# Re-cutting the token groups of a 1040-token input projection into 272, 256 and 512

## The chip, the core and the metric

One core of a Trainium2 chip runs the whole kernel as one program. Its engines are TensorE (PE in the profile; PEld is its weight load, which overlaps the matmuls), VectorE (DVE), ScalarE (ACT), GpSimd (POOL) and SyncE (SP); DVE and ACT do the elementwise work, SP and ACT issue the DMAs. The metric is device time of one execution in microseconds (us): the median of three runs of the kernel before is 1239.22 us (1239.05 to 1239.32).

## The reference

One layer of a hybrid decoder on 16 meta tokens plus 1024 tokens, float32, width 1024. What the change touches is the first product, `z`, and the way its results go on:

```
h = layer_norm(concat(meta, x))                       # 1040 x 1024
z = h @ w_in + b_in                                   # 1040 x 3840
q(512) | k(128) | v(128) | c_val(512) | c_gate(512) | g_attn(1024) | g_conv(1024) = split(z)
y_attn = sliding_window_attention(q, k, v, ...) @ w_attn_proj     # window 128, 16 meta keys, 8 heads, 2 kv heads
c = silu(layer_norm(causal_dwconv31(c_val * sigmoid(c_gate))));  y_conv = c @ w_conv_proj
mixed = sigmoid(g_attn) * y_attn + sigmoid(g_conv) * y_conv
h = layer_norm(ALPHA * h + mixed @ w_out)
u, g = split(causal_dwconv3(h @ ffn_w_up))            # 2 x 2816
out = layer_norm(ALPHA * h + (gelu(g) * u) @ ffn_w_down)[16:]
```

## The kernel before

**The product z.** Every large product is made with split operands: a float32 value is a high part, rounded to the format that TensorE multiplies, and a low part, the rest. One chunk of 128 inputs is three matmuls, high·high, high·low and low·high (lines 300, 304 and 305 in `product`). h0, the normalized input, is kept transposed and split in two arrays, RHO (input chunks 0 to 3) and RHC (4 to 7); `h0(k, hl, a, b)` gives the place of chunk k, part hl, tokens a to b. z has 30 column tiles of 128. The first three (k, v and the first query tile) are made in `z_first` while h0 is still being built; the other 27 go through `z_tile`: eight for the convolution (`conv_chunk`, two for each of four channel blocks), three query tiles, sixteen gate tiles. A tile walks three token groups, HG = 0 to 272, 272 to 656 and 656 to 1040; query and gate tiles use TG, where the first group starts at token 14 and has 258. A group is 8 chunks, 24 matmuls, into one PSUM buffer (`ps_z`, three of them), and is then evacuated: by ACT into a staging place in FA (`stage`: five slots of 400 columns) for gates and queries, by DVE (line 668) into `cin` for the convolution's values. The weights of a tile come by DMA and are split by ACT (line 269) and DVE (line 272).

**Queries.** `q_evac` stages a group, casts it to its high part `qsh` on ACT (line 354), subtracts it on DVE into the low part `qsl` (line 355) and stores both to DRAM (`qd`), the high part by ACT's queue, the low one by SP's. Attention loads them later as `qt`.

**What runs between.** From 55 to 410 us the z tiles share TensorE with attention (scores `ps_s`, transposes `ps_t`, outputs `ps_o`) and the sums of the convolution's layer norm (`ps_m`). DVE does the convolution's 31 taps (line 677), attention's softmax and the evacuations. The order on each engine is set at build time by a scheduler from priorities (`tc.cur_priority`, `rank`) and a few explicit edges (`after`); `ahead` is a z chunk behind which the first attention matmuls are put. After 410 us come the two projections (`ps_p`), the output product (`ps_w`), the ConvFFN's first product (line 1568, matmuls of 258 and 256 columns, weights in `ws` and in parts of RHO) and its second (line 1712, 512 columns). `FA`, `RHC`, `RHO` and `OB` are large arrays whose parts are given new uses as the program goes on.

Of the kernel before, what the change touches and what calls it, by code (L numbers as in the profile page):

```python
# [23 lines left out]
F = mybir.dt.float32  # L24
R = mybir.dt.float32r
AF = mybir.ActivationFunctionType
OP = mybir.AluOpType
AX = mybir.AxisListType

P = 128  # L30
D = 1024
KC = D // P
# [3 lines left out]
U0 = 14  # L36
U = T - U0
HD = 64
NH = 8
NKV = 2  # L40
CW = 512
KW = 208
# [11 lines left out]
HG = [(0, 272), (272, 656), (656, 1040)]  # L54
UG = [(0, 258), (258, 642), (642, 1026)]

PG = [(0, 258), (258, 514), (514, 770), (770, 1026)]


HW = 514  # L60
# [40 lines left out]
def tile_hybrid_layer(  # L101
# [3 lines left out]
    nc = tc.nc  # L105
    PSUM = bass.MemoryType.PSUM

    def dram(ap, offset, dims):
        return bass.AP(tensor=ap.tensor, offset=ap.offset + offset, ap=[list(d) for d in dims])

    def load(o, i):
        return nc.sync.dma_start(out=o, in_=i)
# [5 lines left out]
    def f32(ap):  # L118
        return ap.bitcast(F)
# [19 lines left out]
    arena = ctx.enter_context(tc.tile_pool(name="arena", bufs=1, side="left"))  # L139
    dpool = ctx.enter_context(tc.tile_pool(name="scratch", bufs=1, space=bass.MemoryType.DRAM))  # L140

    FA = arena.tile([P, 6144], F, name="FA")
    RHC = arena.tile([P, 8320], R, name="RHC")
    RHO = arena.tile([P, 8320], R, name="RHO")
    OB = arena.tile([P, 4 * U], F, name="OB")

    v1d = dpool.tile([NH, J_LEN], F, name="v1d")
# [3 lines left out]
    qd = dpool.tile([P, 2 * 4 * U], F, name="qd")  # L151
# [11 lines left out]
    pat = ps_stack.enter_context(tc.tile_pool(name="pat", bufs=1, space=PSUM, reuse_waits="tile"))  # L163

    qsp_stack = ExitStack()
    qsp = qsp_stack.enter_context(tc.tile_pool(name="qsp", bufs=2, side="right", reuse_waits="tile"))
    start = ExitStack()
    sp = start.enter_context(tc.tile_pool(name="start", bufs=1, side="right", reuse_waits="tile"))

# [83 lines left out]


    def h0(k, hl, a, b):
        g = next(g for g, x in enumerate(HG) if a < x[1])
        x, y = HG[g]
        i, n = (k % 4) * 2 + hl, y - x
        o = i * n + ((6144 if i else 0), 272, 3344)[g]
        return (RHO if k < 4 else RHC)[:, o + a - x:o + b - x]  # L260


    tc.cur_priority = RK_QKV
# [28 lines left out]
    chunks_done = []  # L292
# [15 lines left out]
    def z_group(wt, g, a, b, evac):  # L308
        hi, lo = wt
        ps = pat.tile([P, 512], F, name="ps_z", tag="mm", bufs=3)  # L310
        product(ps[:, :b - a], [(hi[:, k], lo[:, k], h0(k, 0, a, b), h0(k, 1, a, b)) for k in range(KC)])
        with rank(RK_EVAC):
            evac(g, a, b, ps[:, :b - a])

    def z_tile(fill, groups, evac, wt=None):
        wt = wt or weights([P, KC, P], fill)
        for g, (a, b) in enumerate(groups):
            z_group(wt, g, a, b, evac)

    def in_cols(m):  # L320
        return lambda raw: load(raw, w_z[m])

    TG = [(a + U0 if i == 0 else a, b) for i, (a, b) in enumerate(HG)]

    st_next = [0]

    def stage(n, lo=4104, cnt=5):
        i = st_next[0] % cnt
        st_next[0] += 1
        return FA[:, lo + i * 400:lo + i * 400 + n]  # L330

    tc.cur_priority = RK_QKV + 1000

# [11 lines left out]
    def q_at(i):  # L345
        return 8 * P * i + 16


    def q_evac(r):
        def evac(g, a, b, ps):  # L350
            t = stage(b - a)
            nc.scalar.activation(t, ps, AF.Identity, bias=qb[:, r:r + 1], scale=HD ** -0.5)
            h, l = (qsp.tile([P, 400], R, name=n, tag=n)[:, :b - a] for n in ("qsh", "qsl"))
            nc.scalar.copy(h, t)
            nc.vector.tensor_tensor(l, t, f32(h), OP.subtract)
            for hl, (put, x) in enumerate(((store, f32(h)), (load, f32(l)))):
                c = 0
                if g == 0:
                    c = 2
                    load(dram(qd, (hl * 4 + r) * 2, [[8 * U, P], [1, 2]]), x[:, :2])  # L360
                n = (b - a - c) // P
                i = (a - U0 + c) // P
                put(dram(qd, q_at(i) + (hl * 4 + r) * HD, [[8 * U, P], [4 * P, 2 * n], [1, HD]]),
                    x[:, c:].rearrange("p (n q) -> p n q", q=HD))
        return evac


    def in_order():
# [256 lines left out]
    wt_c1 = [weights([P, KC, P], in_cols(m)) for m in (11, 7)]  # L625
# [9 lines left out]
    ap = att.enter_context(tc.tile_pool(name="att", bufs=1, side="right", reuse_waits="tile"))  # L635
# [18 lines left out]
    def conv_chunk(c):  # L654
        sig = {}

        def g_evac(g, a, b, ps):
            sig[g] = stage(b - a)

            nc.scalar.activation(sig[g], ps, AF.Tanh, bias=bcol(10 + c), scale=0.5)  # L660
            nc.scalar.activation(sig[g], sig[g], AF.Identity, bias=half_, scale=0.5)

        z_tile(in_cols(10 + c), HG, g_evac, wt_c1[0] if c == 1 else None)
        cin = cp.tile([P, 16 + T], F, name="cin", tag="cin")
        nc.vector.memset(cin[:, 0:16], 0.0)

        def v_evac2(g, a, b, ps):
            nc.vector.scalar_tensor_tensor(cin[:, 16 + a:16 + b], ps, bcol(6 + c), sig[g], OP.add, OP.mult)

        z_tile(in_cols(6 + c), HG, v_evac2, wt_c1[1] if c == 1 else None)  # L670
        with rank(RK_CONV + c * 100):
            for j in range(TAPS):
                wc = cdw[:, j * CH + c:j * CH + c + 1]
                if j == 0:
                    nc.vector.tensor_scalar(acc[c], cin[:, j:j + U], wc, cdwb(c), OP.mult, OP.add)
                else:
                    nc.vector.scalar_tensor_tensor(acc[c], cin[:, j:j + U], wc, acc[c], OP.mult, OP.add)  # L677

    def gate_tile(i):
# [6 lines left out]

        z_tile(in_cols(14 + i), TG, gate_evac)

# [14 lines left out]
    for r in range(2):  # L703
        rows = slice(r * HD, (r + 1) * HD)

        def put(o, j, skew=1):
            load(o[rows], dram(vd, r * J_LEN + j, [[L8 - skew, HD], [2 * J_LEN, NH // 2], [1, o.shape[-1]]]))
# [13 lines left out]
    for q4 in range(2):  # L721
        ps = pat.tile([P, 512], F, name="ps_v4", tag="t", bufs=2)
        for i in range(4):
            c = NMETA + (q4 * 4 + i) * P
            nc.tensor.transpose(ps[:, i * P:(i + 1) * P], vT[:, c:c + P], ident)
        src = ps[:, :].rearrange("p (n g d) -> p n g d", g=2, d=HD)
        for g in range(NKV):
            hi, lo = (V[:, q4 * 4:q4 * 4 + 4, g, i] for i in range(2))
# [10 lines left out]
    for r in range(1, 4):  # L739
        z_tile(in_cols(r), TG, q_evac(r))  # L740

# [13 lines left out]
    tc.cur_priority = RK_Z - 500  # L755
    first_chunk = len(chunks_done)
    gate_tile(0)
    ahead = chunks_done[first_chunk + 2 * KC + 5]

    tc.cur_priority = RK_ATT  # L760

# [3 lines left out]
    for h in range(NH):  # L765
        g, r = divmod(h, 4)
        o = ps[:2, h * 16:(h + 1) * 16]
        after(nc.tensor.matmul(o, pairs0[g][:, 0, r, :], Kx[g][:, 0, 0:16], start=True, stop=False), ahead)
        nc.tensor.matmul(o, pairs0[g][:, 1, r, :], Kx[g][:, 0, 0:16], start=False, stop=True)
    s2 = ap.tile([P, NH, 16], F, name="s2")  # L770
    nc.vector.memset(s2, 0.0)
    w2 = s2[:2]
    nc.vector.tensor_tensor(w2, ps[:2, :P].rearrange("p (h m) -> p h m", m=16), biasq, OP.add)
# [27 lines left out]
    for g in range(NKV):  # L801
# [4 lines left out]
        hi, lo = (t[:16, g * 8:g * 8 + 8].rearrange("p (r q) -> p r q", r=4) for t in p2)  # L806
        nc.scalar.copy(hi, src)
        nc.vector.tensor_tensor(lo, src, f32(hi), OP.subtract)
    for g in range(NKV):
        o = po[:, g * 8:g * 8 + 8]  # L810
# [7 lines left out]
    def weights_out(blocks):  # L818
        a, n = 2 * blocks[0], 2 * len(blocks)
        ps = pat.tile([P, 512], F, name="ps_r", tag="t", bufs=2)  # L820
        nc.tensor.transpose(ps[:4 * n, :P], rall[:, a:a + n].rearrange("p n h -> p (n h)"), ident)
        t = ap.tile([24, P], F, name="rt", tag="rt", bufs=2)
        nc.scalar.copy(t[:4 * n], ps[:4 * n, :P])
        for h in range(NH // 2):
            store(dram(rd, 2 * h * S + a * HD, [[HD, n], [S, 2], [1, HD]]),
                  t[h:4 * n:4].rearrange("p (r q) -> p r q", r=2))
# [5 lines left out]
    for i in range(NB):  # L832
        for g in range(NKV):
            q = load_q(g, i) if i else q0[g]
            s = ap.tile([P, 2, 2, KW], F, name="s", tag="s", bufs=3)
# [5 lines left out]
            for u in range(2):  # L841
# [3 lines left out]
                for h in range(2):  # L845
                    o = ps[:, h * KW:h * KW + w]
# [20 lines left out]
            for h in range(2):  # L867
                for u in range(2):
                    j = h * 2 + u
                    x = s[:, h, u, first[u]:]  # L870
# [6 lines left out]
            for n, cols_of in ((P, (0, 80)), (80, (P, 0))):  # L877
                ps = pat.tile([P, 512], F, name="ps_t", tag="t", bufs=2)
                used = [u for u in range(2) if i or n == 80 or u]
                x = slice(used[0] * 256, 512)  # L880
                for u in used:
                    for h in range(2):
                        c = (u * 2 + h) * P
# [7 lines left out]
            for u in range(2):  # L891
                terms = [(V[:, i - 1 + u, g], P, pts[0])] if i or u else []
                terms.append((VA[:80, 2 * i + u, g], 80, pts[1]))
                x = slice(u * 256, u * 256 + 256)
# [171 lines left out]

    MX_AT = {2: (RHC, 0), 3: (RHC, 1), 6: (RHC, 2), 7: (RHC, 3), 0: (RHO, 0), 4: (RHO, 1), 1: (RHO, 2), 5: (RHO, 3)}

# [64 lines left out]
    for m in range(KC):  # L1133
        hi, lo = weights([P, KC, P], lambda raw: load(raw, w_ab[m]))

        def branch(i, g, tag, bufs):
            a, b = PG[g]
            ps = pat.tile([P, 512], F, name="ps_p", tag=tag, bufs=bufs)
# [6 lines left out]
        def merge(g, psa, psb):  # L1145
            a, b = PG[g]
            n = b - a
# [51 lines left out]
    def quadrant(sub, kk, h):  # L1199
# [3 lines left out]

    B_AT = [[(RHC, 6224), (RHO, 4112), (OA, 16), (RX, 48), (OA, 2096), (OA, 6224), (OA, 4144)],
            [(OC, 48), (OC, 2096), (OC, 4144), (OC, 6192), (RHC, 2096), (RHC, 48), (RHC, 4144)]]
    B11, B21, BT2, BT1, BT3, BT4, B22 = range(7)
# [153 lines left out]

    RING = [RHO[:, i * 1024:(i + 1) * 1024] for i in range(4)]
    RING += [None] * 4
    RING += [RHO[:, 6208 + i * 1024:6208 + (i + 1) * 1024] for i in range(2)]
    ring_next, W2 = [0], []
# [79 lines left out]
    ahead = []  # L1444
# [4 lines left out]
    for i in (3, 7, 2, -1, 6, 0, 4, 1, 5):  # L1449
# [4 lines left out]
        ahead = [None, (i, *rows)] if i == 3 else [(i, *rows)]  # L1454
# [83 lines left out]
    for c in range(FC):  # L1538
# [8 lines left out]
        for subs in passes:  # L1547
            last = subs == passes[-1]
            w_next = iter(range(7))
            a, b = SUB[subs[0]][0], SUB[subs[-1]][1]  # L1550
            i = max(a, 2)
# [96 lines left out]

    F_AT = [(RHC, 6208), (RX, 0), (RHC, 0), (RHO, 0), (RHO, 2048), (RHO, 4096)]
    W_DN = [(OC, 0), (OC, 2048), (OC, 4096), (OC, 6144), (RHC, 2048), (RHC, 4096), (RHO, 6144)]  # L1650

# [215 lines left out]
```

## Time and profile before

| | value |
|---|---|
| median of 3 runs | 1239.22 us (1239.05 to 1239.32) |
| the profiled execution | 1238.92 us |
| its span, first to last instruction | 1237.1 us |
| granted clock of TensorE, mean | 0.999 |
| matmuls | 8539 |
| z tiles of `z_tile` | 27, from 55 to 410 us |
| busy in 55 to 130 us (75): DVE, ACT | 71.2, 23.5 us |
| busy in 200 to 275 us (75): DVE, ACT | 71.2, 46.1 us |

A row of the timeline is the start in us, the length in us, the engine, the line, the operation, what it writes and reads, and its shape. The length of a matmul contains its way through the array; successive matmuls overlap, so that what one costs is the distance of the starts. In the groups view, the first number behind the bar is the busy time in us, the second the mean length in ns.

### The profile page before, as it was taken

The page shows a single profiled execution, that of the slowest core. Times are in us where ns is not written, and L with a number is a line of the kernel's source. Part 1 is how long each engine was busy: PE and PEld are TensorE (multiplying, and loading weights), DVE is VectorE, ACT ScalarE, POOL GpSimd, SP SyncE. Part 2 cuts the span into 40 slices and gives each one's busy share as a digit, 9 for nine tenths or more (in the row PEclk, how much of TensorE's full clock was granted, in tenths as well). Part 3 has the DMA queues.
Part 4 walks back from the last instruction along what each step waited for, and adds up shares of the span by engine and source line. Part 5 has one row for each costly group of instructions (what it writes and reads, how often), then busy time and mean ns, then how long its engine had stood idle before and what let it go on. Part 6 is the DMA issues. An engine that isn't in the chain of part 4 may idle for free.

```text
span 1237.1 us, 21709 instructions
## 1 busy us (share of the span) xinstructions
PE 1226.4 (99%) x8539; PEld 1167.6 (94%) x8539; DVE 1084.2 (88%) x1842; ACT 580.1 (47%) x1048; POOL 16.0 (1%) x25
## 2 busy tenths in 40 slices
PE   9999999999999999999999999999999999999997
PEld 8999999999999999888999999999999998888885
DVE  7899989999978798759899999998999986996697
ACT  7532336654255323344655555455454554544330
POOL 1000000000000010000000000000000000000000
PEclk9999999999999999999999999999999999999999
DMA  7297844412265555222155555554465468987722
GB/s 283 73 297 154 195 115 107 133 36 91 76 164 153 183 147 146 103 86 86 56 176 204 196 189 204 188 179 145 163 211 190 177 244 318 391 314 292 255 86 85
DMA packets 109024, 213.08 MB, mean 172 GB/s; under 512 B 31739, under 2 KB 48683, under 8 KB 108794
## 3 DMA queue, kind: packets, MB, share of 16 engines
q1 hardware_dynamic: 93002, 200.63, 49.2%
q10 hardware_dynamic: 15920, 11.07, 2.9%
q8 instruction: 67, 1.10, 0.4%
q14 instruction: 35, 0.29, 0.1%
HBM read 150.04 MB, written 62.70 MB: 172 GB/s over the span
## 4 chain that ended last, share of the span: by engine, by line
PE 97%; DVE 2%; ACT 0%; issue 0%; DMA 0%; DVEq 0%; SPq 0%
PE px L1568 14%; PE py L1568 9%; PE ps_x L1712 9%; PE ps_z L304 8%; PE ps_z L305 8%; PE ps_z L300 8%; PE ps_z L1712 7%; PE pw L1568 5%; PE pz L1568 5%; PE ps_p L300 2%; PE ps_p L304 2%; PE ps_p L305 2%; PE ps_w L300 2%; PE ps_w L305 2%; PE ps_w L304 2%; PE ps_z L524 2%
## 5 line engine op out<-in xcount | busy, mean ns | idle before, releaser
L677 DVE SCALAR_TENSOR_TENSOR FA<-cin,cols,FA 128x1026 f32<-128x1026 f32 x120 | 152.1, 1278 | 0.9
L305 PE MATMUL ps_z<-RHO,wlo 128*128 128x384 f32 (+2 forms) x324 | 104.1, 321 | 0.0
L300 PE MATMUL ps_z<-RHO,whi 128*128 128x384 f32 (+2 forms) x324 | 103.9, 321 | 0.0
L304 PE MATMUL ps_z<-RHO,whi 128*128 128x384 f32 (+2 forms) x324 | 103.9, 321 | 0.0
L305 PE MATMUL ps_z<-RHC,wlo 128*128 128x384 f32 (+2 forms) x324 | 103.8, 320 | 0.0
L304 PE MATMUL ps_z<-RHC,whi 128*128 128x384 f32 (+2 forms) x324 | 103.7, 320 | 0.0
L300 PE MATMUL ps_z<-RHC,whi 128*128 128x384 f32 (+2 forms) x324 | 103.6, 320 | 0.0
L269 ACT CAST whi<-wr 128x1024 fp32r<-128x1024 f32 x37 | 38.9, 1051 | 91.6 <-PE ps_z L304 71.6
L1377 ACT CAST RHO<-wr 128x512 fp32r<-128x512 f32 x92 | 55.4, 619 | 24.2 <-DVE wr L1395 11.5
L1378 DVE TENSOR_TENSOR RHO<-wr,RHO 128x512 fp32r<-128x512 f32 x92 | 61.9, 684 | 5.0 <-ACT RHO L1377 4.9
L300 PEld LDWEIGHTS ps_z<-RHO,whi 128*128 128x128 f32 x324 | 61.0, 188 | 0.1
L300 PEld LDWEIGHTS ps_z<-RHC,whi 128*128 128x128 f32 x324 | 61.1, 189 | 0.0
L305 PEld LDWEIGHTS ps_z<-RHO,wlo 128*128 128x128 f32 x324 | 61.0, 188 | 0.0
L304 PEld LDWEIGHTS ps_z<-RHO,whi 128*128 128x128 f32 x324 | 61.0, 188 | 0.0
L304 PEld LDWEIGHTS ps_z<-RHC,whi 128*128 128x128 f32 x324 | 61.0, 188 | 0.0
L305 PEld LDWEIGHTS ps_z<-RHC,wlo 128*128 128x128 f32 x324 | 60.9, 188 | 0.0
L1395 DVE TENSOR_TENSOR wr<-wr 128x512 f32<-128x512 f32 x88 | 60.0, 682 | 0.2
L272 DVE TENSOR_TENSOR wlo<-wr,whi 128x1024 fp32r<-128x1024 f32 x35 | 42.7, 1219 | 11.5 <-ACT whi L269 11.1
L684 ACT ACTIVATE FA<-ps_z,cols 128x384 f32<-128x384 f32 (+1 forms) x48 | 26.1, 543 | 47.6 <-PE ps_z L305 42.0
L1580 ACT COPY FA<-px 128x514 f32<-128x514 f32 (+2 forms) x23 | 13.1, 571 | 73.1 <-PE px L1568 73.0
L1377 ACT CAST ws<-wr 128x512 fp32r<-128x512 f32 x60 | 36.3, 619 | 19.1 <-DVE wr L1395 11.8
L1568 PE MATMUL px<-OA,RHO 128*128 128x258 f32 (+1 forms) x336 | 43.8, 279 | 0.0
(475 smaller groups left out, 3477.4 us busy)
## 6 DMA issues: line engine op xcount, KB each, us to landing
wr<-in_w_up_dram SPq DMA_DIRECT2D x44, 512.0 KB, 4.7
wr<-in_w_z_dram SPq DMA_DIRECT2D x30, 512.0 KB, 4.8
fd<-FA SPq DMA_DIRECT2D x44, 256.0 KB, 2.4
OB<-in_w_down_dram SPq DMA_DIRECT2D x19, 512.0 KB
qt<-qd SPq DMA_DIRECT2D x28, 256.0 KB, 4.5
sgd<-FA ACTq DMA_DIRECT2D x32, 192.0 KB, 2.9
td<-OB SPq DMA_DIRECT2D x12, 512.0 KB
sums<-fd SPq DMA_DIRECT2D x12, 512.0 KB, 7.0
```

Source lines behind the costliest of these rows:

```text
L269: ins = nc.scalar.copy(hi, raw)
L272: return (nc.vector if quick else nc.gpsimd).tensor_tensor(lo, raw, f32(hi), OP.subtract)
L300: ins = nc.tensor.matmul(ps, ah, bh, start=i == 0, stop=False)
L304: nc.tensor.matmul(ps, ah, bl, start=False, stop=False)
L305: last = nc.tensor.matmul(ps, al, bh, start=False, stop=i == n - 1)
L677: nc.vector.scalar_tensor_tensor(acc[c], cin[:, j:j + U], wc, acc[c], OP.mult, OP.add)
L684: nc.scalar.activation(t, ps, AF.Tanh, bias=bcol(14 + i), scale=0.5)
L1377: nc.scalar.copy(hi, src)
L1378: ins = nc.vector.tensor_tensor(lo, src, f32(hi), OP.subtract)
L1395: ins = nc.vector.tensor_tensor(*x)
L1568: ins = nc.tensor.matmul(o, x[:, ks], bmat(sub, q, hl, k), start=first and k + j == 0, stop=k == 3 and j == 2, skip_group_check=not first)
L1712: nc.tensor.matmul(banks[i], l[:, ts], r[:, ws], start=first and a and x + k == 0, stop=z and x == len(ops) - 1 and k == 2, skip_group_che ...
```

## The change

The 27 tiles of `z_tile` take the groups ZG = 0 to 272, 272 to 528 and 528 to 1040, so 272 (258 for gates and queries), 256 and 512; h0 is still built in HG, and the first three tiles still use HG. h0's slots are laid out anew: the second and third group of a chunk now stand behind each other (768 columns), the first group's slots begin at column 6196, and RHO and RHC grow from 8320 to 8384 columns. The staging in FA becomes one ring of 2040 columns that hands out just what is asked for. A query group beyond the first is cast, subtracted and stored in parts of at most 256 columns, from three buffers instead of two. s2 shares the ring of the scores `s`, `rt` has one buffer, and `ahead` is two chunks later.

```diff
@@ constants @@
+ZG = [(0, 272), (272, 528), (528, 1040)]
@@ tile_hybrid_layer @@
-    RHC = arena.tile([P, 8320], R, name="RHC")
-    RHO = arena.tile([P, 8320], R, name="RHO")
+    RHC = arena.tile([P, 8384], R, name="RHC")
+    RHO = arena.tile([P, 8384], R, name="RHO")
...
-    qsp = qsp_stack.enter_context(tc.tile_pool(name="qsp", bufs=2, side="right", reuse_waits="tile"))
+    qsp = qsp_stack.enter_context(tc.tile_pool(name="qsp", bufs=3, side="right", reuse_waits="tile"))
...
     def h0(k, hl, a, b):
-        g = next(g for g, x in enumerate(HG) if a < x[1])
-        x, y = HG[g]
-        i, n = (k % 4) * 2 + hl, y - x
-        o = i * n + ((6144 if i else 0), 272, 3344)[g]
-        return (RHO if k < 4 else RHC)[:, o + a - x:o + b - x]
+        i = (k % 4) * 2 + hl
+        o = 6196 + i * 272 if a < 272 else 16 + i * 768 - 272
+        return (RHO if k < 4 else RHC)[:, o + a:o + b]
...
-    TG = [(a + U0 if i == 0 else a, b) for i, (a, b) in enumerate(HG)]
+    TG = [(a + U0 if i == 0 else a, b) for i, (a, b) in enumerate(ZG)]
...
-    def stage(n, lo=4104, cnt=5):
-        i = st_next[0] % cnt
-        st_next[0] += 1
-        return FA[:, lo + i * 400:lo + i * 400 + n]
+    def stage(n):
+        o = st_next[0] if st_next[0] + n <= 2040 else 0
+        st_next[0] = o + n
+        return FA[:, 4104 + o:4104 + o + n]
...
             nc.scalar.activation(t, ps, AF.Identity, bias=qb[:, r:r + 1], scale=HD ** -0.5)
-            h, l = (qsp.tile([P, 400], R, name=n, tag=n)[:, :b - a] for n in ("qsh", "qsl"))
-            nc.scalar.copy(h, t)
-            nc.vector.tensor_tensor(l, t, f32(h), OP.subtract)
-            for hl, (put, x) in enumerate(((store, f32(h)), (load, f32(l)))):
...
+            cut = b - a if g == 0 else 256
+            for x in range(0, b - a, cut):
+                parts_of(r, g, t[:, x:min(b - a, x + cut)], a + x)
         return evac
+
+    def parts_of(r, g, t, a):
+        n = t.shape[-1]
+        h, l = (qsp.tile([P, 272], R, name=x, tag=x)[:, :n] for x in ("qsh", "qsl"))
+        nc.scalar.copy(h, t)
+        nc.vector.tensor_tensor(l, t, f32(h), OP.subtract)
+        for hl, (put, x) in enumerate(((store, f32(h)), (load, f32(l)))):
+            c = 0
+            if g == 0:
+                c = 2
+                load(dram(qd, (hl * 4 + r) * 2, [[8 * U, P], [1, 2]]), x[:, :2])
+            m = (n - c) // P
+            i = (a - U0 + c) // P
+            put(dram(qd, q_at(i) + (hl * 4 + r) * HD, [[8 * U, P], [4 * P, 2 * m], [1, HD]]),
+                x[:, c:].rearrange("p (n q) -> p n q", q=HD))
...
-        z_tile(in_cols(10 + c), HG, g_evac, wt_c1[0] if c == 1 else None)
+        z_tile(in_cols(10 + c), ZG, g_evac, wt_c1[0] if c == 1 else None)
...
-        z_tile(in_cols(6 + c), HG, v_evac2, wt_c1[1] if c == 1 else None)
+        z_tile(in_cols(6 + c), ZG, v_evac2, wt_c1[1] if c == 1 else None)
...
-    ahead = chunks_done[first_chunk + 2 * KC + 5]
+    ahead = chunks_done[first_chunk + 2 * KC + 7]
...
-    s2 = ap.tile([P, NH, 16], F, name="s2")
+    s2 = ap.tile([P, 2, 2, KW], F, name="s2", tag="s", bufs=3)
+    s2 = s2.rearrange("p a b c -> p (a b c)")[:, :NH * 16].rearrange("p (h m) -> p h m", m=16)
...
-        t = ap.tile([24, P], F, name="rt", tag="rt", bufs=2)
+        t = ap.tile([24, P], F, name="rt", tag="rt", bufs=1)
```

TensorE at the first z tile of the convolution, where its first group ends and its second begins, before:

```order
L300 MATMUL ps_z<-RHC,whi 128x272
L304 MATMUL ps_z<-RHC,whi 128x272
L305 MATMUL ps_z<-RHC,wlo 128x272
L300 MATMUL ps_z<-RHO,whi 128x384
L304 MATMUL ps_z<-RHO,whi 128x384
L305 MATMUL ps_z<-RHO,wlo 128x384
```

The same place in the changed kernel:

```order
L299 MATMUL ps_z<-RHC,whi 128x272
L303 MATMUL ps_z<-RHC,whi 128x272
L304 MATMUL ps_z<-RHC,wlo 128x272
L299 MATMUL ps_z<-RHO,whi 128x256
L303 MATMUL ps_z<-RHO,whi 128x256
L304 MATMUL ps_z<-RHO,wlo 128x256
```

And 24 matmuls further on there, where the third group begins (before, a second group of 384 begins at this place):

```order
L299 MATMUL ps_z<-RHC,whi 128x256
L303 MATMUL ps_z<-RHC,whi 128x256
L304 MATMUL ps_z<-RHC,wlo 128x256
L299 MATMUL ps_z<-RHO,whi 128x512
L303 MATMUL ps_z<-RHO,whi 128x512
L304 MATMUL ps_z<-RHO,wlo 128x512
```

The number of matmuls of the tile and their order in it are the same; the widths of the second and third group differ.

ACT at the second group of the first query tile, while h0 is being built (L480 and L488 are the scaling and the cast to the high part of h0's chunks, L352 the query's evacuation, L354 its cast, L343 the evacuation of k), before:

```order
L352 ACTIVATE FA<-ps_z,qb 128x384
L488 CAST RHO<-tm 128x384
L354 CAST qsh<-FA 128x384
L480 ACTIVATE tm<-ps_h_526,cols 128x384
L480 ACTIVATE tm<-ps_h_527,cols 128x384
L116 DMA qd<-qsh 128x6x64
L343 ACTIVATE FA<-ps_z,cols 128x384
L488 CAST RHC<-tm 128x384
L480 ACTIVATE tm<-ps_h_528,cols 128x384
```

The same place now (the lines have moved by 5 to 6, evacuations by −1: L485 for L480, L493 for L488, L360 for L354, L351 for L352):

```order
L351 ACTIVATE FA<-ps_z,qb 128x384
L493 CAST RHO<-tm 128x384
L360 CAST qsh<-FA 128x256
L360 CAST qsh<-FA 128x128
L485 ACTIVATE tm<-ps_h_532,cols 128x384
L485 ACTIVATE tm<-ps_h_533,cols 128x384
L117 DMA qd<-qsh 128x4x64
L117 DMA qd<-qsh 128x2x64
L342 ACTIVATE FA<-ps_z,cols 128x384
L493 CAST RHC<-tm 128x384
L485 ACTIVATE tm<-ps_h_534,cols 128x384
```

One cast more stands ahead of the scaling of the last chunks of h0, and one DMA issue more ahead of k's evacuation.

More of the change, by code (lines that the diff above doesn't have):

```diff
@@ L352, in evac @@
             nc.scalar.activation(t, ps, AF.Identity, bias=qb[:, r:r + 1], scale=HD ** -0.5)
-            h, l = (qsp.tile([P, 400], R, name=n, tag=n)[:, :b - a] for n in ("qsh", "qsl"))
-            nc.scalar.copy(h, t)
-            nc.vector.tensor_tensor(l, t, f32(h), OP.subtract)
-            for hl, (put, x) in enumerate(((store, f32(h)), (load, f32(l)))):
[L357 to L364, printed above, removed]
-        return evac
+            cut = b - a if g == 0 else 256
+            for x in range(0, b - a, cut):
+                parts_of(r, g, t[:, x:min(b - a, x + cut)], a + x)
+        return evac
+    def parts_of(r, g, t, a):
[12 more added lines that the diff above has]
+                x[:, c:].rearrange("p (n q) -> p n q", q=HD))
     def in_order():
```

## The prediction

> **What bounds the kernel now.** I read the page first (busy times, clock, chain), then the waits of PE, the windows by stage, and last the timeline and the longest pieces of the chain for the price of one matmul.
>
> ```profile
> PE 1226.4 (99%) x8539; PEld 1167.6 (94%) x8539; DVE 1084.2 (88%) x1842; ACT 580.1 (47%) x1048; POOL 16.0 (1%) x25
> PEclk9999999999999999999999999999999999999999
> PE 97%; DVE 2%; ACT 0%; issue 0%; DMA 0%; DVEq 0%; SPq 0%
> PE ps_w L548 <- DVE sel L1101: 1.1, 1, 1.1
> PE ps_h L474 <- ACT xn L440: 0.6, 1, 0.6
> PE pw L1568 <- DVE OA L1253: 0.4, 1, 0.4
> PE ps_z L521 <- ACT FA L480: 0.3, 1, 0.3
> ```
>
> TensorE is busy for 1226.4 of 1237.1 us at the full clock in all forty slices, makes 97% of the chain that ended last, and has four waits in all, 2.4 us together. None of them lies between 55 and 410 us, where the 27 z tiles stand that the change touches. There the windows say:
>
> ```profile
> 55.00:130.00 75.00, 75.00 (x485) 74.57 (x484) 71.22 (x85) 23.51 (x40) 0.00 (x0) 1.00 0.78 208
> 130.00:200.00 70.00, 70.00 (x487) 69.43 (x486) 65.22 (x133) 28.90 (x83) 0.00 (x0) 1.00 0.58 151
> 200.00:275.00 75.00, 75.00 (x545) 74.59 (x545) 71.20 (x174) 46.11 (x138) 0.00 (x0) 1.00 0.34 92
> 335.00:410.00 75.00, 75.00 (x487) 75.00 (x486) 60.59 (x122) 38.91 (x60) 0.00 (x0) 1.00 0.58 161
> ```
>
> The columns after the length are PE, PEld, DVE, ACT and POOL. PE is never idle; DVE has 3.8, 4.8, 3.8 and 14.4 us free. So what counts is the time from the start of one matmul to the start of the next ("start to start"), and after that whether DVE can follow a faster PE.
>
> **The group sizes.** Each of 27 tiles has three token groups of 24 matmuls; two groups of 384 become one of 256 and one of 512, and the 258 (272 in the eight conv tiles) stays. The instruction count and the streamed columns stay the same, so a gain can come only from what a matmul costs beyond its columns. First rows of three successive groups, and the groups with the new widths elsewhere in the program:
>
> ```profile
> 364.67 0.34 PE L300 MATMUL ps_z<-RHO,whi 128*128 128x384 f32 x1
> 368.83 0.34 PE L300 MATMUL ps_z<-RHO,whi 128*128 128x384 f32 x1
> 373.35 0.28 PE L300 MATMUL ps_z<-RHO,whi 128*128 128x258 f32 x1
> 376.25 0.34 PE L300 MATMUL ps_z<-RHO,whi 128*128 128x384 f32 x1
> 376.43 0.34 PE L304 MATMUL ps_z<-RHO,whi 128*128 128x384 f32 x1
> ...
> 627.30 2.72 PE px L1568 x24
> 632.74 2.79 PE px L1568 x24
> 1019.41 29.93 PE ps_z L1712 x132
> ...
> L1568 PE MATMUL px<-OC,RHO 128*128 128x256 f32 x312 | 39.6, 276 | 0.0
> L305 PE MATMUL ps_z<-RHO,wlo 128*128 128x384 f32 x216 | 73.2, 339 | 0.0
> ```
>
> The 24 matmuls of 384 take 368.83 − 364.67 = 4.16 us, 173.3 ns each. The 24 of 256 in the FFN's piece at 627.30 take 2.72 us, 113.3 ns each. The 132 of 512 take 29.93 us, 226.7 ns each. Beyond one column per cycle at 2.4 GHz (the 160.0, 106.7 and 213.3 that I reckon with) these are 13.3, 6.6 and 13.4 ns: the narrow one pays half. Two of 384 cost 346.6, a 256 and a 512 cost 340.0: 6.6 ns less. Six rows like the last one, x216 each, are 1296 matmuls of 384, thus 648 pairs: 648 × 6.6 = **−4.3 us**.
>
> The Trainium skill's page "TensorE: Matmul & The Clock Gate", section "Back-to-back issue gap", gives the isolated gap of a warm matmul as N/2.4 plus about 2.5 ns, the same extra for every width. By that rule 256 and 512 cost just what 384 and 384 cost, the term is 0 instead of −4.3, and the time would be 1240.0, 0.8 above before. The trace does not agree on the extra: it shows 13.3 at 384 and 6.6 at 256.
>
> **What a change of width gives back.** In the row pair 376.25 and 376.43 the first 384 after a 258 takes 180 ns by the printed starts, some 7 over the steady 173. No row shows 258, then 256, then 512 in z. For 27 × 3 changes of width at 0 to 20 ns I allow 0 to 1.6 us and take **+0.5**.
>
> **The new places in RHO and RHC.** The first group's slots move from 6144 to 6196 plus multiples of 272, those of the wider groups to 16 plus multiples of 768. Whether the start column matters can be bounded with the 258s: in z 24 of them take 376.25 − 373.35 = 2.90 us, 120.8 ns each, while the piece at 632.74 (258 wide too, with operands elsewhere) takes 116.3. If the new slots bring that price, 456 × 4.5 = −2.1 us. If they are the worse ones, I take the reverse, +2.1. Nothing says which, and the true start columns of before (62, 14, 30 and 46 modulo 64) and of after (50, 2, 18 and 34) interlace, so I take **−0.3**.
>
> **The query parts and the start.** A query group is cast, subtracted and stored in parts of at most 256 columns: one more part for each of the three late query tiles, two more for the first one, which is on its way while h0 is still being built.
>
> ```profile
> 40.38 0.53 ACT L354 CAST qsh<-FA 128x384 fp32r<-128x384 f32 x1
> 49.30 0.79 PE L524 MATMUL ps_z<-RHC,whi 128*128 128x384 f32 x2
> 49.64 0.19 PEld L524 LDWEIGHTS ps_z<-RHC,whi 128*128 128x128 f32 x1 [0.32 <-DVE RHC L491]
> L354 ACT CAST qsh<-FA 128x384 fp32r<-128x384 f32 x8 | 4.1, 517 | 0.2
> L354 ACT CAST qsh<-FA 128x258 fp32r<-128x258 f32 x4 | 1.6, 410 | 0.1
> L355 DVE TENSOR_TENSOR qsl<-FA,qsh 128x384 fp32r<-128x384 f32 x8 | 4.4, 553 | 1.5 <-DMA qd<-qsl 1.5
> L355 DVE TENSOR_TENSOR qsl<-FA,qsh 128x258 fp32r<-128x258 f32 x4 | 1.7, 420 | 0.0
> L116 ACTq DMA_DIRECT2D qd<-qsh x12: 366/372/428, 24.1 to 137.5; - x12
> ```
>
> By the two widths a cast of 256 and one of 128 take about 0.41 + 0.30 us against 0.52 (+0.19), the subtracts 0.42 + 0.28 against 0.55 (+0.15), and one more store is issued on ACT's queue (0.37). Behind them on ACT and DVE stand the casts and subtracts of the last h0 chunks (L488, L491), and for the last chunk PE does wait: the row at 49.64 names DVE RHC L491. So the extra work lands on the path there, in part: 0 to 0.7 us, I take **+0.3**. For the three late query tiles it is 0.19 us on ACT and 0.15 on DVE each, beside 3.8 us of idle DVE in that window: 0. The third qsh/qsl buffer, the shared s ring, the single rt buffer and `ahead` change no work; their cover is the slack below.
>
> **Interrupted groups.** Attention's transposes stand between z matmuls and interrupt some 256 groups, whose price after a transpose no row isolates. I allow 0 to 0.6 us, and take **+0.3**.
>
> **Who can follow.** The evacuations cost the same in sum (three per tile). The waits nearest to PE are these:
>
> ```profile
> 76.73 1.01 DVE L668 SCALAR_TENSOR_TENSOR cin<-ps_z,cols,FA 128x272 f32<-128x272 f32 x2
> 78.65 0.29 PE L300 MATMUL ps_z<-RHO,whi 128*128 128x272 f32 x1
> ...
> 343.67 1.23 DVE L928 TENSOR_TENSOR kx<-csum,c_hi 128x1026 fp32r<-128x1026 f32 x1 [1.12 <-ACT c_hi L927]
> 350.03 0.42 DVE L974 TENSOR_TENSOR FA<-FA,ps_m 128x258 f32<-128x258 f32 x1 [5.13 <-PE ps_m L921]
> ...
> 411.14 0.35 DVE L1025 CAST OA<-OB 128x384 fp32r<-128x384 f32 x1
> 414.00 0.28 PE L300 MATMUL ps_p<-OA,whi 128*128 128x256 f32 x1
> ```
>
> At 78.65 PE takes a ps_z buffer whose evacuation (the first of the two at 76.73) was done 1.4 us before; three tiles further on PE will be about 0.5 us early, which fits. At the means ps_m DVE finished 5.1 us before PE and then waited for it. At 414.00 PE uses a part of OA that was cast 2.5 us before, while DVE in that stretch is itself fed by PE. From the projection on the order of both kernels is the same, so what is saved by 410 us is kept to the end. I count 0.
>
> **Sum.** −4.3 + 0.5 − 0.3 + 0.3 + 0.3 = **−3.5 us**. The profiled execution took 1238.92 us, 0.3 under the median of 1239.22, so it becomes 1235.4, and the median 1239.22 − 3.5 = **1235.7**. A difference of 0.2% (2.5 us) is about what a measurement of this kernel can tell from no change: faster means under 1236.7, slower over 1241.7.
>
> **Rivals.**
>
> ```profile
> 591.50 1.58 PE L1568 MATMUL px<-OC,W 128*128 128x256 f32 x12
> 592.91 1.58 PE L1568 MATMUL pz<-OC,W 128*128 128x256 f32 x12
> 594.33 1.58 PE L1568 MATMUL px<-OC,RHO 128*128 128x256 f32 x12
> ...
> L1568 PE MATMUL px<-OC,ws 128*128 128x256 f32 x204 | 25.9, 276 | 0.0
> L1568 PE MATMUL pz<-OC,RHO 128*128 128x256 f32 x144 | 18.3, 276 | 0.0
> ```
>
> *The 256s stay slow.* Right behind a stretch of 512s the 24 matmuls from 591.50 to 594.33 take 2.83 us, 117.9 ns each, and they keep that for the whole stretch. In the changed z every 256 stands behind a 258 that stands behind 512s. Then 648 × 4.6 = 3.0 us go, and −0.5 is left: **1238.7**. Against it: the FFN, where 256s stand among 258s, has 113.3. Chance 0.15.
>
> *Every width pays the same extra in z.* The 258s of z pay 13.3 ns (120.8 − 107.5) like the 384s. With 120.0 for a 256, 648 × 6.7 = 4.3 us go, and the small losses stay: **1240.0**. Against it: the 113.3 of the FFN's piece. Here lands the rule of the skill as well. Chance 0.06.
>
> *DVE becomes the bound in attention.* It has 3.8 of 75 us free from 200 to 275 us. By 275 us PE is early by 220/355 of 4.3, 2.7 us; if DVE gives none of its free time, that part is lost: **1238.4**. For it: the 95% busy. Against it: much of DVE's work there waits for PE's scores and transposes, so its idle time moves too. Chance 0.04.
>
> *Slower: the FFN's weights lie worse.* RHO grows by 64 columns, and what is packed behind it moves with its parts. Nine rows from px<-OC,RHO x312 to pz<-OC,RHO x144 are 1596 matmuls of 256 in the FFN that read weights there. If the new place puts them at 117.9 instead of 113.3, 1596 × 4.6 = +7.3 and the sum is +3.8: **1243.0**; it decides against the gain from 3.5/1596 = 2.2 ns each. Against it: weights in RHO and in ws cost the same mean, 276. Chance 0.07.
>
> **How the numbers follow.** The forecast has 0.68; its own range, with the slot term from −2.1 to +1.0 and the small losses from nothing to their upper ends, is 1233.6 to 1237.2, and some 0.63 of the 0.68 lies under 1236.7. The rivals at 1238.7, 1240.0 and 1238.4 are within 0.2%, together 0.25. The range 1233.6 to 1240.0 leaves out the slow FFN (0.07) and some 0.05 at both ends. Faster 0.64 (that 0.63 and 0.01 of the DVE case, should it lose less), same 0.28 (0.05 of the forecast, the three rivals, less 0.02 given to either side), slower 0.08 (the FFN's 0.07 and that 0.01).
>
> **What would show it.** Right: 256 groups of z take 2.72 us from first to first row, 512 groups 5.44, tiles 11.0 instead of 11.2; PE's busy time falls by about 3.5 us with no new wait from 55 to 410 us; the FFN pieces stay at 2.72 and 2.79. Wrong: 256 groups of 2.83 us or more; 258 groups off 2.90 by over 0.1; a wait for DVE in the list of PE's waits; FFN pieces of 2.83.

## The result and the profile after

The changed kernel takes 1237.44 us in the median (22 runs, 1237.09 to 1239.56) against 1239.23 for the kernel before: 1.8 us less, a ratio of 0.9987 with a 95% interval of 0.9981 to 0.9993. So it is faster, clear of the interval, by about half of the 3.5 us that were forecast. By the limit that the prediction itself set (under 1236.7 us, 0.2% below before) it is "same", to which it gave 0.28, and not "faster". The execution profiled first was its slowest, 1239.56 us, and lost that time at the start; a second profile of the same kernel (called "again" below) took 1237.57. The windows of the first 55 us, for the kernel before, that first profile and again; the last numbers are the granted clock, the DMA share and GB/s:

```profile
0.00:55.00 55.00, 52.98 (x316) 49.25 (x317) 43.80 (x105) 37.30 (x67) 5.31 (x21) 1.00 0.53 183
```

```profile
0.00:55.00 55.00, 52.17 (x305) 48.59 (x306) 41.47 (x104) 35.91 (x65) 5.31 (x21) 0.97 0.50 171
PE ps_h L479 <- ACT xn L445: 1.4, 1, 1.4
```

```profile
0.00:55.00 55.00, 52.40 (x314) 49.07 (x314) 43.21 (x105) 36.99 (x68) 5.31 (x21) 1.00 0.51 178
PE ps_h L479 <- ACT xn L445: 1.2, 1, 1.2
PE 1224.6 (99%) x8539; PEld 1139.4 (92%) x8539; DVE 1085.1 (88%) x1847; ACT 580.5 (47%) x1053; POOL 15.9 (1%) x25
```

In the first profile TensorE was granted 0.97 there and its first z_tile matmul started at 57.9 us; again it started at 56.1, before at 55.5. So the middle of the program is read from again. PE's busy time in it is 1224.6 instead of 1226.4 us: 1.8 less, as the medians say. PEld falls from 1167.6 to 1139.4 us, which is no gain of its own: a weight load of z takes 188 ns in the mean in both profiles, but between the matmuls of 512 the loads no longer overlap one another.

The windows of again, for the four stretches that were shown of before and for the FFN's first product:

```profile
55.00:130.00 75.00, 75.00 (x496) 68.17 (x496) 72.62 (x91) 24.37 (x43) 0.00 (x0) 1.00 0.78 213
130.00:200.00 70.00, 70.00 (x483) 64.04 (x482) 64.18 (x131) 28.05 (x83) 0.00 (x0) 1.00 0.58 149
200.00:275.00 75.00, 75.00 (x543) 70.39 (x543) 72.89 (x178) 45.63 (x131) 0.00 (x0) 1.00 0.34 92
335.00:410.00 75.00, 75.00 (x491) 68.66 (x490) 61.41 (x123) 39.13 (x60) 0.00 (x0) 1.00 0.55 164
605.00:1019.00 414.00, 413.63 (x3590) 413.26 (x3589) 388.51 (x635) 223.09 (x367) 0.00 (x0) 1.00 0.52 184
```

and the last of these stretches in the kernel before:

```profile
605.00:1019.00 414.00, 413.62 (x3591) 413.30 (x3591) 389.04 (x635) 224.26 (x368) 0.00 (x0) 1.00 0.52 183
```

PE is still never idle from 55 to 410 us, and DVE is busier from 200 to 275 (72.9 of 75 us) without becoming the bound. The first product of the FFN keeps its pace: 3590 matmuls in the window, 3591 before. From the first matmul of the projections to the end it is 830.0 us in again and 830.1 before, so what z saves is kept.

What the groups cost, by the first rows of successive groups of again: a tile without interruption, the next tile's start, the first 512s of the tile in detail, and a 256 group in attention's stretch. A group is called undisturbed when no other matmul stands between its 24. The rows are printed to 0.01 us, so a price from one group is good to some 0.4 ns.

```profile
315.00 0.29 PE L299 MATMUL ps_z<-RHO,whi 128*128 128x258 f32 x1
317.88 0.28 PE L299 MATMUL ps_z<-RHO,whi 128*128 128x256 f32 x1
320.60 0.39 PE L299 MATMUL ps_z<-RHO,whi 128*128 128x512 f32 x1
326.10 0.29 PE L299 MATMUL ps_z<-RHO,whi 128*128 128x258 f32 x1
...
320.60 0.39 PE L299 MATMUL ps_z<-RHO,whi 128*128 128x512 f32 x1
320.83 0.39 PE L303 MATMUL ps_z<-RHO,whi 128*128 128x512 f32 x1
321.06 0.39 PE L304 MATMUL ps_z<-RHO,wlo 128*128 128x512 f32 x1
321.29 0.39 PE L299 MATMUL ps_z<-RHO,whi 128*128 128x512 f32 x1
...
277.61 0.28 PE L299 MATMUL ps_z<-RHO,whi 128*128 128x256 f32 x1
280.43 0.40 PE L299 MATMUL ps_z<-RHO,whi 128*128 128x512 f32 x1
```

The 256s take 2.72 us, 113.3 ns each, as forecast. The 512s take 5.50 us, 229.2 ns each, not 226.7; the three of a chunk take 0.69 us (320.60 to 321.29). And the 256 group at 277.61 takes 2.82 us, 117.5 each: the dearer price that 256s have behind the output product exists here too. In again 16 of the 27 groups of 256 have a median distance of starts of 113 or 114 ns and 11 one of 117 or 118; all the slow ones but one start between 150 and 305 us, where attention's matmuls stand between.

Added up over all their starts, the matmuls of z_tile take 307.1 us before (258s 55.6, 272s 24.5, 384s 227.0) and 304.7 in again (55.0, 24.5, 256s 75.3, 512s 149.9). Attention's scores, transposes and outputs take 0.5 us more than before. Between the first z_tile matmul and the first of the projections lie 351.5 us before and 349.7 in again.

### The profile page after: what moved, and what is told of

It reads as the page before. It is cut to its first block, busy times and chain, and to the rows that moved or that the text cites. A ratio compares the mean times of both kernels' runs of the same rounds, so it can differ in the third digit from the quotient of the medians.

```text
span 1237.7 us, 21739 instructions
## 1 busy us (share of the span) xinstructions
PE 1226.3 (99%) x8539; PEld 1140.5 (92%) x8539; DVE 1084.8 (88%) x1847; ACT 580.9 (47%) x1053; POOL 16.0 (1%) x25
## 4 chain that ended last, share of the span: by engine, by line
PE 97%; DVE 2%; ACT 0%; DMA 0%; issue 0%; SPq 0%; DVEq 0%; ACTq 0%
PE px L1574 14%; PE py L1574 9%; PE ps_x L1718 9%; PE ps_z L304 8%; PE ps_z L303 8%; PE ps_z L299 8%; PE ps_z L1718 7%; PE pw L1574 5%; PE pz L1574 5%; PE ps_p L299 2%; PE ps_p L304 2%; PE ps_p L303 2%; PE ps_w L303 2%; PE ps_w L299 2%; PE ps_w L304 2%; PE ps_z L529 2%
## 5 line engine op out<-in xcount | busy, mean ns | idle before, releaser
L304 PE MATMUL ps_z<-RHO,wlo 128*128 128x256 f32 (+2 forms) x324 | 103.5, 320 | 0.0
L303 PE MATMUL ps_z<-RHO,whi 128*128 128x256 f32 (+2 forms) x324 | 103.4, 319 | 0.0
L304 PE MATMUL ps_z<-RHC,wlo 128*128 128x256 f32 (+2 forms) x324 | 103.4, 319 | 0.0
L303 PE MATMUL ps_z<-RHC,whi 128*128 128x256 f32 (+2 forms) x324 | 103.4, 319 | 0.0
L299 PE MATMUL ps_z<-RHO,whi 128*128 128x256 f32 (+2 forms) x324 | 103.3, 319 | 0.0
L299 PE MATMUL ps_z<-RHC,whi 128*128 128x256 f32 (+2 forms) x324 | 103.2, 319 | 0.0
L1383 ACT CAST RHO<-wr 128x512 fp32r<-128x512 f32 x92 | 55.4, 619 | 23.1 <-DVE wr L1401 12.0
L1586 ACT COPY FA<-px 128x514 f32<-128x514 f32 (+2 forms) x23 | 13.1, 571 | 73.0 <-PE px L1574 72.9
L689 ACT ACTIVATE FA<-ps_z,cols 128x258 f32<-128x258 f32 (+2 forms) x48 | 26.1, 544 | 39.4 <-PE ps_z L304 36.6
L1384 DVE TENSOR_TENSOR ws<-wr,ws 128x512 fp32r<-128x512 f32 x60 | 40.4, 684 | 4.1 <-ACT ws L1383 4.0
```

Of the source, the lines that this page charges most:

```text
L299: ins = nc.tensor.matmul(ps, ah, bh, start=i == 0, stop=False)
L303: nc.tensor.matmul(ps, ah, bl, start=False, stop=False)
L304: last = nc.tensor.matmul(ps, al, bh, start=False, stop=i == n - 1)
L689: nc.scalar.activation(t, ps, AF.Tanh, bias=bcol(14 + i), scale=0.5)
L1384: ins = nc.vector.tensor_tensor(lo, src, f32(hi), OP.subtract)
```

## The experiments

All were run in the same manner as the changed kernel, with the kernel before beside them (1239.2 us each time); a time is the median of 11 executions, of 6 at column 8. Diffs are against the changed kernel. A start is named by its column in a period of 64 (256 bytes): by the addresses in the built program RHO and RHC themselves begin at column 48 of it, so that 16 + 768i is column 0. That the period is 64 is read from the 258s, whose prices repeat every four slots (4 × 272 is 17 × 64).

**The same kernel again.**

> The changed kernel once more, for a second profile of it (the first one has its TensorE clock at 0.97 over the first 55 us). Expected 1237.4 us, within 0.4. In z the 24 matmuls of 512 should again take 5.50 us (229.1 ns each: 226, 229, 232 in turn), those of 256 mostly 2.72. If the forecast's price of 226.7 for a 512 were right and the first profile odd, 5.44 us and the same time.

Measured 1237.36 us (ratio 0.9986, 0.9977 to 0.9995), and the 5.50 us just shown. The forecast's price of a 512 did not hold in z.

**The group sizes alone undone.**

```diff
-ZG = [(0, 272), (272, 528), (528, 1040)]
+ZG = [(0, 272), (272, 656), (656, 1040)]
```

> The group sizes alone undone: 272 (258), 384 and 384, with the new slots, ring and query parts. Theory A, the sizes bring the gain and the rest next to nothing: 384s at 173 to 175 ns again, 1239.0 us (before, less 0.6 for the 258s' slots, and 0.4 for the start). Rival B, the gain comes from the slots, the ring or the third buffer: 1237.4 us stays, or less.

Measured 1238.91 us (0.9999, 0.9991 to 1.0008), as theory A said, and the first rows

```profile
387.24 0.34 PE L299 MATMUL ps_z<-RHO,whi 128*128 128x384 f32 x1
391.40 0.34 PE L299 MATMUL ps_z<-RHO,whi 128*128 128x384 f32 x1
395.56 0.28 PE L299 MATMUL ps_z<-RHO,whi 128*128 128x258 f32 x1
```

give 4.16 us again, 173.3 ns for a 384. Beside the other edits the sizes bring 1.5 us; what those edits bring alone, 0.3 us, is within the interval.

**The wide slots at column 48.**

```diff
-        o = 6196 + i * 272 if a < 272 else 16 + i * 768 - 272
+        o = 6196 + i * 272 if a < 272 else i * 768 - 272
```

> The wide groups' slots start at 768i instead of 16 + 768i, so that their rows start 48 columns into the period of 64, where the 512s of the later products start, instead of 0. Theory A, the start column sets the price of a 512 in z: 226.7 instead of 229.1 ns, 648 x 2.4 = -1.6 us, 1235.9 us. Rival B, it is the two weights and three products of a chunk, or what stands between: the 512s stay at 229 and the time at 1237.4.

Measured 1239.46 us (1.0003, 0.9994 to 1.0012): 2.1 us slower than the changed kernel. The rows show both halves of it:

```profile
387.98 0.28 PE L299 MATMUL ps_z<-RHO,whi 128*128 128x256 f32 x1
390.85 0.40 PE L299 MATMUL ps_z<-RHO,whi 128*128 128x512 f32 x1
396.32 0.28 PE L299 MATMUL ps_z<-RHO,whi 128*128 128x258 f32 x1
...
395.19 0.39 PE L303 MATMUL ps_z<-RHC,whi 128*128 128x512 f32 x1
395.41 0.39 PE L304 MATMUL ps_z<-RHC,wlo 128*128 128x512 f32 x1
395.64 0.39 PE L299 MATMUL ps_z<-RHC,whi 128*128 128x512 f32 x1
395.87 0.39 PE L303 MATMUL ps_z<-RHC,whi 128*128 128x512 f32 x1
```

Three steps of the 512s from 395.19 to 395.87 take 0.68 us, 226.7 each, as theory A said. But the first six of such a group are dearer, some 231 ns in the mean, so that the whole group takes 5.47 us, 227.9 each, and over all starts the 512s save 0.6 us (149.9 to 149.3) of the 1.6 expected. And the 24 matmuls of 256 now take 2.87 us, 119.6 each, all over z (the median distance is 120 ns in each of the 27 groups): that was not expected, and it costs 2.9 us (75.3 to 78.2), more than the 512s give.

**The wide slots at columns 32, 16, 4, 8 and 56.** The same line with 48, 32, 20, 24 and 8 in place of 16.

> The wide groups' slots start at 48 + 768i: their rows start 32 columns into the period of 64, where the 256s of the projections and the FFN start. Theory A, the start column alone sets the price, and 32 serves both widths: 256s at 113.3, 512s at 226.7 instead of 229.1 ns, -1.6 us, 1235.8 us. Rival B, a 512 is cheap only at 48, where alone the program has it: 512s at 229, 1237.4 us. Rival C, 256s are slow at every start but 0: 120 ns, 1239.5 us.

> The wide groups' slots start at 32 + 768i: 16 columns into the period. Theory A, multiples of 32 are good for a 256, odd multiples of 16 cost it 6.7 ns and suit a 512: 256s at 120, 512s at 226.7, the time of the slots at 48 columns into the period, 1239.5 us. Rival C, 16 is like 0: 1237.4 us.

> The wide groups' slots start at 20 + 768i, 4 columns into the period. Theory A, the price depends on the start column more finely than by 16; 0 gave 113.3 and 229.1 ns, 16 gave 119 and 231.5, so something between, 342 to 351 ns for a 256 and a 512: 1237.4 to 1241.2 us. Rival B, a start off a multiple of 16 makes the 512 as cheap as at 48 (226.7) and leaves the 256 at 113.3: 1235.9 us.

> The same at 24 + 768i, 8 columns into the period. Theory A, between the prices at 0 and at 16: 1237.4 to 1241.2 us. Rival B, cheaper than at 0: 1235.9 us.

> The same at 8 + 768i, 56 columns into the period. Theory A, between the prices at 48 (120 and 226.7 ns) and at 0 (113.3 and 229.1): 1237.4 to 1239.5 us. Rival B, the good half of both (113.3 and 226.7): 1235.9 us.

First rows of successive groups at column 32, then at column 8:

```profile
388.36 0.28 PE L299 MATMUL ps_z<-RHO,whi 128*128 128x256 f32 x1
391.08 0.39 PE L299 MATMUL ps_z<-RHO,whi 128*128 128x512 f32 x1
396.68 0.28 PE L299 MATMUL ps_z<-RHO,whi 128*128 128x258 f32 x1
```

```profile
391.07 0.28 PE L299 MATMUL ps_z<-RHO,whi 128*128 128x256 f32 x1
393.95 0.40 PE L299 MATMUL ps_z<-RHO,whi 128*128 128x512 f32 x1
399.55 0.28 PE L299 MATMUL ps_z<-RHO,whi 128*128 128x258 f32 x1
```

Column 32 leaves the 256 at 113.3 (2.72 us) and makes the 512 dearer, 233.3 (5.60). Column 8 makes both dear, 120.0 and 233.3. All places, each by such rows, with the median time:

| first column | 256, ns | 512, ns | sum, ns | time, us (ratio to before) |
|---|---|---|---|---|
| 0 (the change) | 113.3 | 229.2 | 342.5 | 1237.36 (0.9986) |
| 4 | 118.3 | 231.3 | 349.6 | 1240.58 (1.001) |
| 8 | 120.0 | 233.3 | 353.3 | 1242.95 (1.003) |
| 16 | 118.3 | 232.5 | 350.8 | 1241.23 (1.0016) |
| 32 | 113.3 | 233.3 | 346.6 | 1239.76 (1.0003) |
| 48 | 119.6 | 227.9 | 347.5 | 1239.46 (1.0003) |
| 56 | 116.7 | 233.3 | 350.0 | 1240.62 (1.0012) |

The times largely follow the sums. They follow still better the 256s and 512s added up over all their starts: 225.2 us at column 0, then 228.6, 230.7, 229.3, 227.7, 227.5 and 228.8 down the table, so that the times differ from that of column 0 by these differences to 0.3 us. In its numbers theory A held only at 4: at 32 the 512 is dearer than even rival B had it, 16 is not like 48, and neither 8 nor the 512 at 56 lies between its neighbours. What is left of it is that the start column changes the price, with nothing else changed. Column 0 is the best of the seven, and none makes both widths cheap.

**The old groups at column 32.** The old sizes and `48 + i * 768 - 272`.

> The old groups (two of 384) in the slots that start 32 columns into the period. Theory A, a 384 costs 173.3 there as at 0 (it has 13.3 over its columns at both): 1238.9 us. Rival D, the start column was what made the 384s dear: some 2.4 to 6 ns less each, 3 to 8 us less, 1231 to 1236 us, and the new group sizes would be beside the point.

Measured 1240.87 us (1.0011, 1.0002 to 1.002), and the first rows

```profile
388.91 0.34 PE L299 MATMUL ps_z<-RHO,whi 128*128 128x384 f32 x1
393.10 0.34 PE L299 MATMUL ps_z<-RHO,whi 128*128 128x384 f32 x1
397.29 0.28 PE L299 MATMUL ps_z<-RHO,whi 128*128 128x258 f32 x1
```

give 4.19 us, 174.6 ns for a 384, 1.3 more than at column 0, where theory A had the same price at both. The time is 2.0 us above that of the old sizes at column 0. So the 384s stood better before, and rival D falls.

**The first groups' slots.**

```diff
-        o = 6196 + i * 272 if a < 272 else 16 + i * 768 - 272
+        o = 6160 + i * 272 if a < 272 else 16 + i * 768 - 272
```

> The first groups' slots at 6160 instead of 6196, so that the 258s and 272s start at the columns of the period that they had before (14, 30, 46, 62 and 0, 16, 32, 48). Theory A, the new places bring the 258s 1.2 ns each and the 272s nothing: 456 x 1.2 = 0.5 us more, 1237.9 us. Rival B, they bring nothing: 1237.4 us.

Measured 1238.66 us (0.9994, 0.9985 to 1.0002), 1.3 us more. The rows of a 258 group and the next one,

```profile
384.45 0.28 PE L299 MATMUL ps_z<-RHO,whi 128*128 128x258 f32 x1
387.36 0.28 PE L299 MATMUL ps_z<-RHO,whi 128*128 128x256 f32 x1
```

give 2.91 us against 2.88 in again. Over all starts the 258s take 55.5 instead of 55.0 us, as theory A said. Another 0.6 us goes to the 256s (75.9 instead of 75.3): 16 of their groups have the dearer price instead of 11, with nothing changed about them. What picks the price is not settled. Here the first four groups, from 59 to 94 us, are among the dear ones, though no matmul of attention is near. With the first groups at their old columns the new sizes are thus only 0.5 us under the kernel before, within the interval.

**512 ahead of 256.**

```diff
-ZG = [(0, 272), (272, 528), (528, 1040)]
+ZG = [(0, 272), (272, 784), (784, 1040)]
```

> The second group has 512 tokens and the third 256: a 256 then stands right behind 512s and ahead of the next tile's 258s. Theory A, what sets a 256 off in its slower state (118 instead of 113.3) is an interruption by other matmuls of the group or just ahead of it, and it stays so to the group's end; the order of the widths does not matter: about as many slow groups as in the changed kernel (12 of 27), 1237.4 us. Rival B, 256s behind 512s are slow, as behind the output product: all 27 groups at 118, 15 x 24 x 4.6 = 1.7 us more, 1239.1 us.

Measured 1238.24 us (0.9992, 0.9983 to 1.0001).

```profile
375.57 0.39 PE L299 MATMUL ps_z<-RHO,whi 128*128 128x512 f32 x1
381.06 0.28 PE L299 MATMUL ps_z<-RHO,whi 128*128 128x256 f32 x1
383.79 0.29 PE L299 MATMUL ps_z<-RHO,whi 128*128 128x258 f32 x1
```

Here a 256 group right behind 512s takes 2.73 us: 113.8 each. Of the 14 undisturbed ones 10 are fast, so "slow behind 512s" falls as a rule. The 0.8 us over the changed kernel shows in the 258s (55.7 instead of 55.0 us), the 272s (24.7 instead of 24.5) and the 256s (75.8 instead of 75.3; 16 groups are dear), less what the 512s lose (149.2 instead of 149.9).

**The first query tile in whole parts.**

```diff
-    qsp = qsp_stack.enter_context(tc.tile_pool(name="qsp", bufs=3, side="right", reuse_waits="tile"))
+    qsp = qsp_stack.enter_context(tc.tile_pool(name="qsp", bufs=2, side="right", reuse_waits="tile"))
...
-            cut = b - a if g == 0 else 256
+            cut = b - a if g == 0 or r == 0 else 256
...
-        h, l = (qsp.tile([P, 272], R, name=x, tag=x)[:, :n] for x in ("qsh", "qsl"))
+        h, l = (qsp.tile([P, 384], R, name=x, tag=x)[:, :n] for x in ("qsh", "qsl"))
```

> The first query tile's second and third group in one part of 384 again (two buffers of 384 instead of three of 272), all else as in the changed kernel. Theory A, the extra cast, subtract and store in the first 55 us cost 0.3 us (0 to 0.7): 1237.1 us, and the windows of PE before 49.6 us as in the kernel before. Rival B, they are hidden: 1237.4 us.

Measured 1237.69 us (0.9988, 0.9979 to 0.9997), 0.3 over again, so not faster: rival B is the nearer one. That the extra parts cost nothing is not shown. The first z_tile matmul starts at 55.4 us in this profile and at 55.5 before, against 55.6 to 56.1 in the eleven other profiles with the parts (the first one of the change, 57.9, aside), so a cost of 0.1 to 0.3 us at the start stays possible, and z itself happens to take 0.2 us more here.

## Why the prediction was right, and by how much its terms missed

The direction and its reason hold: with the sizes undone, most of the gain is gone. The range held the time, 1233.6 to 1240.0, but only by the part that had been added for the rivals: the forecast's own range ended at 1237.2. That range was also too narrow for its own terms, whose ends add up to 1232.8 to 1238.8. The forecast was 1235.7, and the sum broke like this:

| term | forecast, us | by the runs, us |
|---|---|---|
| widths at their undisturbed price | −4.3 | −2.7 |
| change of width, interrupted groups, slow 256s | +0.8 | +1.4 |
| first groups' slots | −0.3 | −0.6 |
| start | +0.3 | 0 to +0.3, not resolved |
| sum | −3.5 | −1.9 to −1.6 |

**The price of a 512** is the step that was mis-sized. It was taken from the last product, 226.7 ns, where the rows start at column 48; in z they start at 0 and take 229.2. 648 × 2.5 = 1.6 us of the gain went there. The run with slots at 48 shows that the column has a part in it: there the 512s come down to 226.7 behind the first six of a group, and to 227.9 over the whole group. Why the start column matters was not found; it was only varied. The part on the places in RHO had weighed the start column for the 258s alone. That the 256s came out at the forecast 113.3 was luck in this respect: the price was taken from the FFN, where the rows start at column 32, and 0 happens to share it. At 4, 8, 16, 48 and 56 a 256 takes 116.7 to 120.0, and the same change would have gained nothing (1239.5 to 1243.0 us).

**The disturbed groups** were put at 0.8. By the starts, the 256s take 1.9 us over 113.3 each (75.3 − 73.4), the 512s 1.4 over 229.2 (149.9 − 148.5), attention's own matmuls 0.5 more; the 384s had 2.4 over 173.3 in the kernel before (227.0 − 224.6). That is 1.4 more than before (1.9 + 1.4 + 0.5 − 2.4). Most of the 256s' part is the rival "the 256s stay slow", which came true for 11 groups of 27: 11 × 24 × 4.5 = 1.2 us.

**The slots** brought 0.6 in the matmuls of the first groups, inside the bounds of 2.1 either way. But the terms do not simply add: with the first groups at their old columns the change gains 0.5 us (the run at 6160), without the sizes 0.3, whole 1.8. Of the 1.0 that is missing between them some 0.6 are the five more groups of 256 that had the dear price at 6160, and why they had it is open, so that part of the gain is luck. **The start** cost between nothing and 0.3, which these runs do not settle.

Of the signs that the prediction named, the 256 groups of 2.72 us are there in 16 of 27, the 512 groups take 5.50 instead of 5.44, and a tile takes 11.10 us (315.00 to 326.10) instead of 11.0. PE's busy time fell by 1.8 us instead of 3.5, with no new wait from 55 to 410 us.

**The rivals.** "Every width pays the same extra": false at column 0, where a 256 pays 6.6 ns and a 512 15.9 over its columns, yet nearly true at 48 (120.0 and, behind the first six, 226.7 are 13.3 and 13.4 over). Thus the rule of the Trainium skill's page "TensorE: Matmul & The Clock Gate", section "Back-to-back issue gap", N/2.4 plus about 2.5 ns for an isolated matmul, gives neither of the two extras here, and its form, one constant for all widths, nearly holds at only one of the seven starts: at 48 it makes the new sizes worth nothing, and the time there was that of before (1.0003). **DVE** had room: its 72.9 us in the tightest window still let PE run without a gap. **The FFN's weights** behind the grown RHO cost the same: 3590 and 3591 matmuls in the same window.

The Trainium skill's page "SBUF — State Buffer", section "Operand start alignment", asks for a start at a multiple of the element size and says that it is about what is legal, not about speed. All starts here are legal; between them a pair of a 256 and a 512 differs by up to 10.8 ns, and the kernel by 5.6 us.

## What to carry to other kernels

In a stream of matmuls without gaps, a price per matmul is a price at a start column: before one is carried from one stage to another, compare the columns at which the moving rows start, and the neighbours, not the width alone. A gain of a few ns per matmul is of the size of these effects, so such a change is best tried with several places for the operand. And an undisturbed group's price has to be summed with that of the interrupted ones, which here took 1.4 of the 2.7 us that the prices left.

## What the hardware showed that was not expected

The start column of the moving operand changes what a matmul takes from start to start: a 256 from 113.3 to 120.0 ns, a 512 from 227.9 (226.7 behind the first six of a group) to 233.3, and what is good for the one is not for the other. A 256 at column 0 has two prices, 113.3 and 118 ns, that mostly last for a whole group of 24. In the changed kernel it is nearly always the dearer one where attention's matmuls stand between, but that is not the cause by itself: with the first groups' slots at 6160 four groups at 59 to 94 us have it too, far from attention. The 512s at column 0 take 226, 229 and 232 ns in turn over a chunk's three products.
